# Odd channel tiles read in place, weight parts split one product ahead, and the last stores queued behind loads

## The chip, the cores and the metric

One core of one Trainium2 chip runs the kernel alone. The metric is the device time of one execution in microseconds (us), as the median of several runs.

## The reference

The reference is one decoder block in float32: attention and a gated recurrence side by side, an output projection, and an MLP with a squared ReLU. The change touches the MLP only:

```python
D_MODEL, SEQ, D_FF = 2048, 512, 8192
...
f = relu(h2 @ w_ff1) ** 2        # h2: 512 x 2048, the second norm's scaled output
x = x + gate2 * (f @ w_ff2)
```

## The kernel before

Every float32 product is made of three matmuls on values split into a high and a low part: high x high, high x low and low x high. A low part is `src - hi`; ACT casts the high one, DVE subtracts. `h2[k]` is the pair of high and low parts of channel tile k (128 channels x 512 tokens), k = 0 to 15, and `uT[k]` is the same tile unsplit. Both lie in SBUF.

The MLP's first 2048 hidden channels are computed plainly, in four groups (`first_hidden`, `hidden`), up to about 1190 us. All else is done in a form of Strassen's that needs seven products of half matrices in place of eight. For this the operands are stored in DRAM as seven *forms*: the quarters of `h2` and of `f`, and four sums of quarters. `input_forms` makes those of `h2` and `make_forms` those of `f`; each form has a high and a low half, in `h_hid` and `h_lod`, `f_hid` and `f_lod`. These stores are issued on POOL's queue (L1030).

Stage 1 computes the remaining hidden channels in six blocks of 1024 (b = 2 to 7), each of seven products numbered 1 to 7. Their order is 1, 5, 6, 7, 3, 4, 2; in the first block it is 1, 3, 5, 6, 7, 4, 2. Stage 2 multiplies `f` by `w_ff2` in two halves q of the output and four parts c, again seven products each. A product (`product`) is 48 matmuls of 128x512 into two PSUM banks: four steps u, each with 12 matmuls on one pair of weight parts `vhi`, `vlo`. `operand` fetches the other side's form, `Fh` and `Fl`, as two loads of 512 KB each for the high and for the low half, on POOL's queue from pools of four buffers each (L1097). For products 4 and 2 of stage 1 it loads four tiles of 1 MB (`Rh`, `Rl`) once and keeps them.

The weights come as `raw` tiles on SP's queue. `part` makes, where a product needs one, a difference of two raw tiles on DVE (L1129), casts it on ACT (`vhi`, L1145) and takes the low part on DVE (`vlo`, L1146):

```python
for u in range(KG):
    with tc.high_priority() if early else ExitStack():
        ws = part(i, u, w, first)
    mm(u, *ws, range(2))
    tick()
```

Each u has one buffer for its `vhi` and one for its `vlo`. After a product, `combine` adds its banks into the sums `s` (DVE L1204 to L1216, copies on ACT). `turn` transposes a finished group of f, applies the squared ReLU and stores its forms. In stage 2 the first part of each half copies the banks to `a` on ACT; behind the last copy, `residual_in` issues a `gate` load and eight `d` loads on ACT's queue.

A scheduler merges this program text into one order per engine, by priority; each engine runs its order in sequence. POOL's queue has eight lanes: an issue waits until the transfer issued eight before has landed.

Of the kernel before, what the change touches and what calls it, by code (L numbers as in the profile page):

```python
# [44 lines left out]
def hybrid_block(ctx, tc, x, c, positions, norm1_w, w_ada, b_ada, w_in, q_norm_w, k_norm_w,  # L45
# [177 lines left out]
    ph = ctx.enter_context(ExitStack())  # L223
    hp = ph.enter_context(tc.tile_pool(name="hp", bufs=1, side="right"))
# [15 lines left out]
    for i in range(NK):  # L240
        pair(i)
# [25 lines left out]
    spare.extend(hp.tile([P, 512], F32, name="araw", tag=f"{c}{k}") for k in range(8, NK) for c in ("hi", "lo"))  # L267
# [742 lines left out]
    def forms_in_dram(name, n):  # L1010
        return [dr.tile([n * FORMS * P, 512], F32, name=f"{name}_{c}d").rearrange("(g i p) n -> g i p n", i=FORMS, p=P)
                for c in ("hi", "lo")]

    fparts, hparts = forms_in_dram("f", NG), forms_in_dram("h", KG)

    def make_forms(fs, dst, g, stage, in_place=False):
# [7 lines left out]
        for a, b in ((0, 2), (2, 4), (4, 6), (6, 7)):  # L1024
            hi = stage()[:, 0:b - a]
            lo = fs[:, a:b].bitcast(F32R) if in_place else stage()[:, 0:b - a]
            act.copy(hi, fs[:, a:b])
            dve.tensor_tensor(lo, fs[:, a:b], hi.bitcast(F32), op=ALU.subtract)
            for d, t in zip(dst, (hi, lo)):
                pool.dma_start(d[g, a:b].rearrange("i p n -> p i n"), t.rearrange("p i a t -> p i (a t)").bitcast(F32))  # L1030
            yield
# [23 lines left out]
    for g in range(PLAIN):  # L1055
# [5 lines left out]
        for j, r in enumerate(rs):  # L1061
            dve.tensor_tensor(block(fs, j), halves(r), halves(r), op=ALU.mult)
# [9 lines left out]
    ph.close()  # L1072
# [307 lines left out]
```

## Time and profile before

| | us |
|---|---|
| median of 3 runs | 2312.09 (2311.49 to 2312.19) |
| profiled execution | 2306.17 |
| its span | 2304.4 |
| TensorE busy | 2230.5 (97%) |
| VectorE (DVE) busy | 1825.9 (79%) |
| ScalarE (ACT) busy | 1103.0 (48%) |
| mean granted clock | 0.994 |

Busy time is summed over the instructions of an engine. A timeline row gives start, duration, engine, source line, what is written and read, and in brackets the idle time ahead with what ended it. A chain of rows with `x3` has three instructions in one row. The clock is 1 at TensorE's upper level, 2.4 GHz, and a half at 1.2 GHz.

### The profile page before, as it was taken

Reading aid. Unit: us, or ns where it says so; the run is one execution under the profiler, and the core shown is the slowest. Engines: PE = TensorE matmul, PEld = TensorE weight load, DVE = VectorE, ACT = ScalarE, POOL = GpSimd, SP = SyncE. Lnnn points to the kernel's source line nnn. Section 1 sums busy time; section 2 is a strip of 40 time slices with the busy share of each in tenths; the row PEclk is TensorE's granted clock in tenths of the full one; section 3 lists DMA queues with packets and bytes.
Section 4 is the critical chain, followed back from the end, with each engine's and each line's share of the span. In section 5 each row is a group of like instructions: output and inputs, shape, how many; then the busy total and the mean of one; then the engine's idle time right before and its main releaser. Section 6 shows DMA issues by size and latency. Waiting matters only on the chain.

```text
span 2304.4 us, 33163 instructions
## 1 busy us (share of the span) xinstructions
PE 2230.5 (97%) x11769; PEld 1829.2 (79%) x11769; DVE 1825.9 (79%) x2773; ACT 1103.0 (48%) x1958; POOL 458.1 (20%) x668
## 2 busy tenths in 40 slices
PE   4999999999999999999999999999998999999999
PEld 3787877888778888888887888888887888888887
DVE  6899777677776565669767988988895789967878
ACT  5555434433344553457644555565563333344332
POOL 1000022000230000001332323323232222222221
PEclk9999999999999999999999999999999999999999
DMA  9798455556545256746999799889889987999784
GB/s 327 249 337 314 123 176 156 176 162 215 178 149 182 74 186 218 259 132 220 366 382 382 252 341 355 301 297 380 310 295 369 339 288 262 364 336 335 277 302 165
DMA packets 264695, 606.71 MB, mean 263 GB/s; under 512 B 23284, under 2 KB 44032, under 8 KB 264528
## 3 DMA queue, kind: packets, MB, share of 16 engines
q1 hardware_dynamic: 186800, 332.54, 42.8%
q0 software_dynamic: 72832, 262.60, 31.1%
q10 hardware_dynamic: 4896, 9.44, 1.2%
q8 instruction: 93, 1.52, 0.3%
q14 instruction: 74, 0.61, 0.1%
HBM read 522.68 MB, written 81.81 MB: 262 GB/s over the span
## 4 chain that ended last, share of the span: by engine, by line
PE 56%; DMA 16%; DVE 14%; issue 10%; POOL 2%; ACT 1%; SPq 0%; DVEq 0%; POOLq 0%; ACTq 0%
PE f L1160 9%; PE f L1161 9%; PE f L1159 9%; DMA araw<-in_w_ada_dram 7%; PE prj L198 4%; PE prj L200 4%; PE prj L199 4%; DMA f_lod<-fs 3%; DVE acc L129 3%; PE f L208 2%; PE f L206 2%; PE f L207 2%; DVE vlo L1146 2%; DVE wlo L40 2%; PE prj L206 2%
## 5 line engine op out<-in xcount | busy, mean ns | idle before, releaser
L1145 ACT CAST vhi<-raw 128x1024 fp32r<-128x1024 f32 x392 | 412.8, 1055 | 547.1 <-PE f L1161 434.3
L1146 DVE TENSOR_TENSOR vlo<-raw,vhi 128x1024 fp32r<-128x1024 f32 x392 | 477.4, 1225 | 154.3 <-ACT vhi L1145 153.5
L1159 PE MATMUL f<-vhi,Fh 128*128 128x512 f32 x1376 | 537.6, 391 | 8.3 <-DMA Fh<-h_hid 3.6
L1160 PE MATMUL f<-vlo,Fh 128*128 128x512 f32 x1376 | 538.1, 391 | 3.0 <-DVE vlo L1146 3.0
L1161 PE MATMUL f<-vhi,Fl 128*128 128x512 f32 x1376 | 537.2, 390 | 2.1 <-DMA Fl<-f_lod 1.3
L39 ACT CAST whi<-wraw 128x512 fp32r<-128x512 f32 (+1 forms) x368 | 219.8, 601 | 449.3 <-PE prj L200 323.7
L198 PE MATMUL prj<-whi,hi 128*128 128x512 f32 x896 | 365.0, 407 | 1.3 <-ACT gg L698 1.3
L200 PE MATMUL prj<-whi,lo 128*128 128x512 f32 x896 | 351.5, 392 | 0.0
L199 PE MATMUL prj<-wlo,hi 128*128 128x512 f32 x896 | 350.8, 391 | 0.0
L40 DVE TENSOR_TENSOR wlo<-wraw,whi 128x512 fp32r<-128x512 f32 (+1 forms) x368 | 245.1, 670 | 111.7 <-ACT whi L39 107.1
L129 DVE SCALAR_TENSOR_TENSOR acc<-araw,sc,acc 128x512 f32<-128x512 f32 (+1 forms) x392 | 253.9, 678 | 98.5 <-DMA araw<-in_w_ada_dram 97.2
L1159 PEld LDWEIGHTS f<-vhi,Fh 128*128 128x128 f32 x1376 | 259.0, 188 | 63.3 <-issue 7.1
L1160 PEld LDWEIGHTS f<-vlo,Fh 128*128 128x128 f32 x1376 | 259.0, 188 | 61.7 <-DVE vlo L1146 8.3
L1161 PEld LDWEIGHTS f<-vhi,Fl 128*128 128x128 f32 x1376 | 259.1, 188 | 56.7 <-DMA Fl<-f_lod 1.8
L1129 DVE TENSOR_TENSOR raw<-raw,raw 128x1024 f32<-128x1024 f32 x224 | 269.5, 1223 | 1.8 <-DMA raw<-in_w_ff_dram 1.5
L198 PEld LDWEIGHTS prj<-whi,hi 128*128 128x128 f32 x896 | 169.4, 189 | 36.5 <-ACT gg L698 1.6
L200 PEld LDWEIGHTS prj<-whi,lo 128*128 128x128 f32 x896 | 168.9, 188 | 36.8
L199 PEld LDWEIGHTS prj<-wlo,hi 128*128 128x128 f32 x896 | 169.6, 189 | 32.4 <-DVE wlo L40 0.4
L1097 POOL DMA_DIRECT2D Fh<-f_hid x112 | 80.9, 722 | 428.3 <-PE f L1161 414.8
L208 PE MATMUL f<-hi,wlo 128*128 128x512 f32 x256 | 99.8, 390 | 0.6 <-DVE wlo L40 0.6
L206 PE MATMUL f<-hi,whi 128*128 128x512 f32 x256 | 100.2, 391 | 0.0
L207 PE MATMUL f<-lo,whi 128*128 128x512 f32 x256 | 99.6, 389 | 0.0
(306 smaller groups left out, 2956.9 us busy)
## 6 DMA issues: line engine op xcount, KB each, us to landing
raw<-in_w_ff_dram SPq DMA_DIRECT2D x224, 512.0 KB, 10.0
araw<-in_w_ada_dram SPq DMA_DIRECT2D x384, 256.0 KB, 4.3
Fh<-f_hid POOLq DMA_DIRECT2D x112, 512.0 KB, 6.5
Fl<-f_lod POOLq DMA_DIRECT2D x112, 512.0 KB, 7.4
wraw<-in_w_in_dram SPq DMA_DIRECT2D x104, 512.0 KB, 4.1
Fh<-h_hid POOLq DMA_DIRECT2D x60, 512.0 KB, 6.8
Fl<-h_lod POOLq DMA_DIRECT2D x60, 512.0 KB, 8.3
f_hid<-part POOLq DMA_DIRECT2D x48, 512.0 KB, 8.1
```

What stands on the lines that cost most here:

```text
L39: nc.scalar.copy(hi, src)
L40: (eng or nc.vector).tensor_tensor(lo, src, hi.bitcast(F32), op=ALU.subtract)
L129: dve.scalar_tensor_tensor(acc, raw[:, k - k0], vec[:, k:k + 1], acc, op0=ALU.mult, op1=ALU.add)
L198: pe.matmul(banks[ti], lhsT=hi[:, ts], rhs=whi, start=first, stop=False)
L199: pe.matmul(banks[ti], lhsT=hi[:, ts], rhs=wlo, start=False, stop=False)
L200: pe.matmul(banks[ti], lhsT=lo[:, ts], rhs=whi, start=False, stop=last)
L1129: dve.tensor_tensor(dst, a, b, op=ALU.subtract)
L1145: act.copy(hi, src)
L1146: split_done.append(dve.tensor_tensor(lo, src, hi.bitcast(F32), op=ALU.subtract))
L1159: pe.matmul(banks[t], lhsT=fh[u][:, a, ts], rhs=whi[:, a], start=first, stop=False)
L1160: pe.matmul(banks[t], lhsT=fh[u][:, a, ts], rhs=wlo[:, a], start=False, stop=False)
L1161: pe.matmul(banks[t], lhsT=fl[u][:, a, ts], rhs=whi[:, a], start=False, stop=end)
```

## The change

Four things are done. The odd tiles of `h2` stay in SBUF (pool `hp1`) and products 4 and 2 of stage 1 read them there; the `R` tiles and their loads are gone. The forms of `h2` are made another way: of its quarters only one is stored, from the even tiles of `h2`, and the sums are taken by DVE out of `uT`, so the 16 copies on ACT go. The squares of the plain groups move from DVE to ACT. Last, one list of products (`items`) runs through both stages: inside each product the weight parts of the next one are split for u = 0 to 2 (`ahead`) and the fourth after the last product's combine; and the stores of the last turned group (`behind`) are issued after the operand loads that stand there.

```diff
@@ -220,8 +220,10 @@
...
-    ph = ctx.enter_context(ExitStack())
-    hp = ph.enter_context(tc.tile_pool(name="hp", bufs=1, side="right"))
+    ph1 = ctx.enter_context(ExitStack())
+    ph0 = ctx.enter_context(ExitStack())
+    hp1 = ph1.enter_context(tc.tile_pool(name="hp1", bufs=1, side="right"))
+    hp0 = ph0.enter_context(tc.tile_pool(name="hp0", bufs=1, side="right"))
...
-        return [hp.tile([P, S], F32R, name=f"{c}{i}", tag=f"{c}{i}") for c in ("hi", "lo")]
+        return [(hp0, hp1)[i % 2].tile([P, S], F32R, name=f"{c}{i}", tag=f"{c}{i}") for c in ("hi", "lo")]
...
-    for i in range(NK):
+    for i in (*range(0, NK, 2), *range(1, NK, 2)):
         pair(i)
...
@@ -1007,13 +1010,23 @@
...
-    fparts, hparts = forms_in_dram("f", NG), forms_in_dram("h", KG)
-
-    def make_forms(fs, dst, g, stage, in_place=False):
+    fparts, hparts = forms_in_dram("f", NG), forms_in_dram("h", KG, 8)
+
+    def split_out(fs, a, b, stage, in_place, dst, behind=None):
+
+        hi = stage()[:, 0:b - a]
+        lo = fs[:, a:b].bitcast(F32R) if in_place else stage()[:, 0:b - a]
+        act.copy(hi, fs[:, a:b])
+        dve.tensor_tensor(lo, fs[:, a:b], hi.bitcast(F32), op=ALU.subtract)
+        with tc.issue_after(behind[-1].ins) if behind else ExitStack():
+            for d, t in zip(dst, (hi, lo)):
+                pool.dma_start(d.rearrange("i p n -> p i n"), t.rearrange("p i a t -> p i (a t)").bitcast(F32))
+
+    def make_forms(fs, dst, g, stage, in_place=False, behind=None):
 
         a21, a11, a22, a12, s1, s2, s4 = (fs[:, i] for i in range(FORMS))
         dve.tensor_tensor(s1, a21, a22, op=ALU.add)
@@ -1022,12 +1035,7 @@
         dve.tensor_tensor(s4, a12, s2, op=ALU.subtract)
         yield
         for a, b in ((0, 2), (2, 4), (4, 6), (6, 7)):
-            hi = stage()[:, 0:b - a]
-            lo = fs[:, a:b].bitcast(F32R) if in_place else stage()[:, 0:b - a]
-            act.copy(hi, fs[:, a:b])
-            dve.tensor_tensor(lo, fs[:, a:b], hi.bitcast(F32), op=ALU.subtract)
-            for d, t in zip(dst, (hi, lo)):
...
     def plain_stage():
-        return stg.tile([P, 2, 2, 256], F32R, name="part", bufs=7)
...
     def input_forms(u):
-        fs = plain_forms()
-        for j in range(4):
-            act.copy(block(fs, j), halves(uT[4 * u + j]))
-        yield
-        yield from make_forms(fs, hparts, u, plain_stage)
+
+        xf = stg.tile([P, 4, 2, 256], F32, name="xf", bufs=1)
+        s1, s2, s4, s3 = (xf[:, i] for i in range(4))
+        for a in range(2):
+            ev, od = (halves(uT[4 * u + 2 * a + e]) for e in range(2))
+            a21, a11, a22, a12 = ev[:, 0], ev[:, 1], od[:, 0], od[:, 1]
+            dve.tensor_tensor(s1[:, a], a21, a22, op=ALU.add)
+            dve.tensor_tensor(s3[:, a], a11, a21, op=ALU.subtract)
+            dve.tensor_tensor(s2[:, a], s1[:, a], a11, op=ALU.subtract)
+            dve.tensor_tensor(s4[:, a], a12, s2[:, a], op=ALU.subtract)
+            for d, t in zip(hparts, h2[4 * u + 2 * a]):
+                pool.dma_start(d[u, 1, :, a * 256:(a + 1) * 256], t[:, 256:512].bitcast(F32))
+        yield
+        for a in (0, 2):
+            split_out(xf, a, a + 2, plain_stage, False, [d[u, 4 + a:6 + a] for d in hparts])
+            yield
...
         for j, r in enumerate(rs):
-            dve.tensor_tensor(block(fs, j), halves(r), halves(r), op=ALU.mult)
+            act.activation(block(fs, j), halves(r), AF.Square)
...
-    ph.close()
+    ph0.close()
...
     NC = NG // KG
-    kept = {}
 
     def operand(src, c, i):
 
-        def load(t, d, g):
-            n = t.shape[1]
-            pool.dma_start(t.rearrange("p g a t -> p g (a t)").bitcast(F32),
-                           d[g:g + n, slot_of[i]].rearrange("g p n -> p g n"))
-            return t
-
         if src is hparts and i in (4, 2):
-            if i not in kept:
-                kept[i] = [load(res.tile([P, KG, 2, 256], F32R, name=f"R{n}{i}"), d, 0) for d, n in zip(src, "hl")]
-            return [[t[:, u] for u in range(KG)] for t in kept[i]]
+            half = slice(256, 512) if i == 2 else slice(0, 256)
+            return [[[h2[4 * u + 2 * a + 1][j][:, half] for a in range(2)] for u in range(KG)] for j in range(2)]
         out_ = [[], []]
         for h in range(0, KG, 2):
             for o, d, n in zip(out_, src, "hl"):
-                t = load(pools["fp"].tile([P, 2, 2, 256], F32R, name=f"F{n}"), d, KG * c + h)
-                o.extend(t[:, u] for u in range(2))
+                t = pools["fp"].tile([P, 2, 2, 256], F32R, name=f"F{n}")
+                g = KG * c + h
+                slot_ = (hslot_of if src is hparts else slot_of)[i]
+                loads.append(pool.dma_start(t.rearrange("p g a t -> p g (a t)").bitcast(F32),
+                                            d[g:g + 2, slot_].rearrange("g p n -> p g n")))
+                o.extend([t[:, u, a] for a in range(2)] for u in range(2))
         return out_
 
     def weights(view, g0, c0, order):
...
-    def product(i, src, c, w, tag, by_tile, first, early):
+    def product(i, src, c, ws, tag, by_tile, nxt):
+
 
         banks = [bank("f2", tag=tag) for _ in range(2)]
         fh, fl = operand(src, c, i)
+        ahead = []
...
-                    pe.matmul(banks[t], lhsT=fh[u][:, a, ts], rhs=whi[:, a], start=first, stop=False)
-                    pe.matmul(banks[t], lhsT=fh[u][:, a, ts], rhs=wlo[:, a], start=False, stop=False)
-                    pe.matmul(banks[t], lhsT=fl[u][:, a, ts], rhs=whi[:, a], start=False, stop=end)
+                    pe.matmul(banks[t], lhsT=fh[u][a][:, ts], rhs=whi[:, a], start=first, stop=False)
+                    pe.matmul(banks[t], lhsT=fh[u][a][:, ts], rhs=wlo[:, a], start=False, stop=False)
+                    pe.matmul(banks[t], lhsT=fl[u][a][:, ts], rhs=whi[:, a], start=False, stop=end)
 
         if by_tile:
-            ws = [part(i, u, w, first) for u in range(KG)]
             for t in range(2):
                 for u in range(KG):
                     mm(u, *ws[u], (t,))
         else:
             for u in range(KG):
-                with tc.high_priority() if early else ExitStack():
-                    ws = part(i, u, w, first)
-                mm(u, *ws, range(2))
-                tick()
-        return banks
+                mm(u, *ws[u], range(2))
+                if u == KG - 1 or src is hparts:
+                    tick()
+                if nxt and u < KG - 1:
+                    ahead.append(nxt(u))
+        return banks, ahead
...
-        yield from make_forms(fs, fparts, 2 * b + n, stage, True)
+        yield from make_forms(fs, fparts, 2 * b + n, stage, True, loads if 2 * b + n == NG - 2 else None)
...
+    def part_of(item):
+
+        stage_, blk, j, i = item
+        if j == 0:
+            part_of.w = weights(ff1_s, 0, blk * 1024, order_of(item)) if stage_ == 1 else \
+                weights(ff2_s, blk[1] * KG, blk[0] * 1024, order)
+        w, first = part_of.w, blk == PLAIN // 2
+
+        def call(u):
+            with tc.high_priority() if first and j < 2 else ExitStack():
+                return part(i, u, w, first)
+        return call
+
+    def order_of(item):
+        return first_order if item[1] == PLAIN // 2 else order
+
+    items = [(1, b, j, i) for b in range(PLAIN // 2, NG // 2) for j, i in enumerate(order_of((1, b)))]
+    items += [(2, (q, c), j, i) for q in range(2) for c in range(NC) for j, i in enumerate(order)]
...
+    call = part_of(items[0])
+    ws = [call(u) for u in range(KG)]
+    for item, following in zip(items, items[1:] + [None]):
+        stage_, blk, j, i = item
+        first = blk == PLAIN // 2
+        if j == 0 and stage_ == 1 and not first:
+            before, cs, third = cs, after(cs), None
...
+            ph1.close()
+            late = ctx.enter_context(tc.tile_pool(name="late", bufs=1, side="right", reuse_waits="tile"))
...
+        if stage_ == 1:
+            banks, ahead = product(i, hparts, 0, ws, "bg" if first and j < 2 else "mm", False, call)
+            if i == 5 and not first:
+                turned(blk - 1, 0, before)
+            if first and i == 3:
+                third = banks
+            else:
                 for t in range(2):
...
+        else:
+            q, c = blk
+            banks, ahead = product(i, fparts, c, ws, "mm", i == 2 and c == NC - 1, call)
+            if q + c == 0 and i == 5:
+                turned(NG // 2 - 1, 0, cs)
+            for t in range(2):
+                if c == 0:
+                    done = act.copy(accs7[i, t], banks[t])
+                elif c < NC - 1:
+                    dve.tensor_tensor(accs7[i, t], accs7[i, t], banks[t], op=ALU.add)
+                else:
+                    finish(q, i, t, banks[t])
+            if c == 0 and i == 2:
                 with tc.issue_after(done.ins):
                     residual_in(q)
+        if following:
+            ws = ahead + [call(u) for u in range(len(ahead), KG)]
```

Three places show how the orders move. The first is POOL's order at the start of stage 1. `part` is a staged half of a form of f from the last plain group, `Fh` and `Fl` are operand loads, and the first eight of those belong to products 1 and 3. Before:

```order
L1097 DMA Fl<-h_lod 128x2x512
L1097 DMA Rh_12618<-h_hid 128x4x512
L1097 DMA Rl_12620<-h_lod 128x4x512
L1097 DMA Rh_12721<-h_hid 128x4x512
L1097 DMA Rl_12723<-h_lod 128x4x512
L1030 DMA f_hid<-part 128x2x512 x2
L1030 DMA f_lod<-part 128x2x512
L1030 DMA f_hid<-part 128x2x512
L1030 DMA f_lod<-part 128x2x512
L1030 DMA f_hid<-part 128x512
L1030 DMA f_lod<-part 128x2x512
L1097 DMA Fh<-h_hid 128x2x512
```

and now:

```order
L1122 DMA Fh<-h_hid 128x2x512
L1122 DMA Fl<-h_lod 128x2x512
L1027 DMA f_hid<-part 128x2x512
L1122 DMA Fh<-h_hid 128x2x512
L1122 DMA Fl<-h_lod 128x2x512
L1027 DMA f_hid<-part 128x2x512
L1027 DMA f_lod<-part 128x2x512 x2
L1027 DMA f_hid<-part 128x2x512
L1122 DMA Fh<-h_hid 128x2x512
L1122 DMA Fl<-h_lod 128x2x512
L1122 DMA Fh<-h_hid 128x2x512
```

The four `R` loads are gone, and one store, in place of seven, stands ahead of the pair that product 5 asks for first.

The second place is DVE's order in the first block, around product 7 and the following product 4. The numbers name tiles: `f_12530` and `f_12531` are product 7's banks before, `f_12518` and `f_12519` those of now; `vlo<-raw_12188`, `12190`, `12192`, `12194` are product 4's four low parts before, `raw_12156`, `12158`, `12160`, `12162` now. Before:

```order
L1129 TENSOR_TENSOR raw_12194<-raw_12194,raw_12218 128x1024
L1146 TENSOR_TENSOR vlo<-raw_12210,vhi 128x1024
L1146 TENSOR_TENSOR vlo<-raw_12188,vhi 128x1024
L1146 TENSOR_TENSOR vlo<-raw_12190,vhi 128x1024
L1146 TENSOR_TENSOR vlo<-raw_12192,vhi 128x1024
L1206 TENSOR_TENSOR s_12162<-s_12160,f_12530 128x512
L1206 TENSOR_TENSOR s_12163<-s_12161,f_12531 128x512
L1207 TENSOR_TENSOR s_12160<-s_12160,s_12146 128x512
L1207 TENSOR_TENSOR s_12161<-s_12161,s_12147 128x512
L1146 TENSOR_TENSOR vlo<-raw_12194,vhi 128x1024
L1208 TENSOR_TENSOR s_12146<-s_12146,s_12162 128x512
L1210 TENSOR_TENSOR s_12160<-s_12160,f_12296 128x512
```

and now:

```order
L1223 TENSOR_TENSOR s_12133<-s_12131,f_12518 128x512
L1161 TENSOR_TENSOR vlo<-raw_12156,vhi 128x1024
L1223 TENSOR_TENSOR s_12134<-s_12132,f_12519 128x512
L1224 TENSOR_TENSOR s_12131<-s_12131,s_12117 128x512
L1161 TENSOR_TENSOR vlo<-raw_12158,vhi 128x1024
L1144 TENSOR_TENSOR raw_12160<-raw_12160,raw_12184 128x1024
L1224 TENSOR_TENSOR s_12132<-s_12132,s_12118 128x512
L1225 TENSOR_TENSOR s_12117<-s_12117,s_12133 128x512
L1227 TENSOR_TENSOR s_12131<-s_12131,f_12280 128x512
L1144 TENSOR_TENSOR raw_12162<-raw_12162,raw_12186 128x1024
L1161 TENSOR_TENSOR vlo<-raw_12180,vhi 128x1024
L1225 TENSOR_TENSOR s_12118<-s_12118,s_12134 128x512
```

Three of the four low parts stood ahead of the combine that reads product 7's bank; now all four stand behind it, among the combines, the raw sums and the low parts of product 2 (`raw_12180` is one). The third, `vlo<-raw_12160`, follows two rows after the last one shown, behind one more combine.

The third place is POOL's order at the start of stage 2, with the stores of the last turned group (`part` and `fs`). Before:

```order
L1030 DMA f_hid<-part_16446 128x2x512
L1030 DMA f_hid<-part_16468 128x2x512
L1097 DMA Fh<-f_hid 128x2x512
L1097 DMA Fl<-f_lod 128x2x512
L1030 DMA f_lod<-fs_16369 128x2x512
L1030 DMA f_hid<-part_16490 128x2x512
L1030 DMA f_hid<-part_16524 128x512
L1030 DMA f_lod<-fs_16369 128x2x512 x2
L1030 DMA f_lod<-fs_16369 128x512
L1097 DMA Fh<-f_hid 128x2x512
L1097 DMA Fl<-f_lod 128x2x512
```

and now:

```order
L1027 DMA f_hid<-part_16532 128x2x512
L1027 DMA f_hid<-part_16616 128x2x512
L1122 DMA Fh<-f_hid 128x2x512
L1122 DMA Fl<-f_lod 128x2x512
L1027 DMA f_lod<-fs_16344 128x2x512 x2
L1122 DMA Fh<-f_hid 128x2x512
L1122 DMA Fl<-f_lod 128x2x512
L1027 DMA f_hid<-part_16698 128x2x512
L1027 DMA f_lod<-fs_16344 128x2x512
L1122 DMA Fh<-f_hid 128x2x512
L1122 DMA Fl<-f_lod 128x2x512
```

The group's stores, which stood together ahead of a pair of loads, now stand between the pairs.

## Rows read from the trace of the kernel before

**Rows 1.** The page, part 1: busy us, share of the span, instructions.

```profile
PE 2230.5 (97%) x11769; PEld 1829.2 (79%) x11769; DVE 1825.9 (79%) x2773; ACT 1103.0 (48%) x1958; POOL 458.1 (20%) x668
```

**Rows 2.** Windows: length, busy PE PEld DVE ACT POOL, PEclk, DMA share, GB/s.

```profile
1080.00:1189.80 109.80, 109.80 (x486) 90.93 (x485) 73.48 (x100) 58.56 (x90) 43.01 (x63) 1.00 1.00 373
1189.80:1290.00 100.20, 95.80 (x421) 78.44 (x420) 86.18 (x88) 48.85 (x56) 28.98 (x41) 0.98 0.96 356
...
1735.00:1776.00 41.00, 34.24 (x141) 27.00 (x140) 19.36 (x17) 15.12 (x18) 9.38 (x13) 0.96 1.04 392
```

**Rows 3.** Timeline of PE, 1207 to 1221 us: start, us, engine, line, operation.

```profile
1207.74 0.39 PE L1160 MATMUL f<-vlo,Fh 128*128 128x512 f32 x1
...
1211.37 0.39 PE L1161 MATMUL f<-vhi,Fl 128*128 128x512 f32 x1
1215.34 0.47 PE L1159 MATMUL f<-vhi,Fh 128*128 128x512 f32 x1 [3.58 <-DMA Fh<-h_hid]
...
1216.85 0.79 PE L1161 MATMUL f<-vhi,Fl 128*128 128x512 f32 x1 [0.81 <-DMA Fl<-h_lod]
...
1220.56 0.40 PE L1161 MATMUL f<-vhi,Fl 128*128 128x512 f32 x1
```

**Rows 4.** Timeline of POOL (DMA issues), 1178 to 1216 us.

```profile
1183.03 0.77 POOL L1097 DMA_DIRECT2D Rh<-h_hid  x1 [0.71 <-DMA Fh<-h_hid]
...
1190.29 0.75 POOL L1097 DMA_DIRECT2D Rl<-h_lod  x1 [1.96 <-PE f L208]
1195.58 0.71 POOL L1030 DMA_DIRECT2D f_hid<-part  x1 [4.54 <-ACT part L1027]
...
1206.00 0.73 POOL L1097 DMA_DIRECT2D Fh<-h_hid  x1 [1.95 <-DMA Rl<-h_lod]
1207.17 0.73 POOL L1097 DMA_DIRECT2D Fl<-h_lod  x1 [0.44 <-issue]
```

**Rows 5.** Waits of PE, 1080 to 1800 us: total, times, longest.

```profile
PE f L1160 <- DVE vlo L1146: 3.0, 7, 0.8
```

**Rows 6.** Timeline of PE at a block boundary of stage 1.

```profile
1291.68 0.50 PE L1160 MATMUL f<-vlo,Fh 128*128 128x512 f32 x1 [0.35 <-DVE vlo L1146]
```

**Rows 7.** Timeline of PE, 1738 to 1751 us.

```profile
1740.34 0.39 PE L1161 MATMUL f<-vhi,Fl 128*128 128x512 f32 x1
...
1745.46 0.50 PE L1161 MATMUL f<-vhi,Fl 128*128 128x512 f32 x1 [1.32 <-DMA Fl<-f_lod]
...
1749.16 0.44 PE L1161 MATMUL f<-vhi,Fl 128*128 128x512 f32 x1
```

**Rows 8.** Timeline of PE, 1769 to 1776 us.

```profile
1773.36 0.49 PE L1159 MATMUL f<-vhi,Fh 128*128 128x512 f32 x1 [1.96 <-ACT vhi L1145]
1774.62 0.50 PE L1160 MATMUL f<-vlo,Fh 128*128 128x512 f32 x1 [0.77 <-DVE vlo L1146]
```

**Rows 9.** Timeline of ACT and of its DMA issues (ACTq), 1760 to 1776 us.

```profile
1763.42 0.33 ACTq L1272 DMA_DIRECT2D gate<-gate  x1
...
1772.26 3.90 ACT L1145 CAST vhi<-raw 128x1024 fp32r<-128x1024 f32 x4 [8.39 <-DMA Fl<-f_lod]
```

**Rows 10.** Timeline of DVE, 1216 to 1253 us.

```profile
1217.61 1.23 DVE L1146 TENSOR_TENSOR vlo<-raw,vhi 128x1024 fp32r<-128x1024 f32 x1
...
1222.15 1.23 DVE L1146 TENSOR_TENSOR vlo<-raw,vhi 128x1024 fp32r<-128x1024 f32 x1
...
1245.55 3.49 DVE L1146 TENSOR_TENSOR vlo<-raw,vhi 128x1024 fp32r<-128x1024 f32 x3
...
1250.50 1.28 DVE L1206 TENSOR_TENSOR s<-s,f 128x512 f32<-128x512 f32 x2
1251.69 1.29 DVE L1207 TENSOR_TENSOR s<-s,s 128x512 f32<-128x512 f32 x2
```

**Rows 11.** Timeline of POOL, 1712 to 1745 us.

```profile
1732.05 0.73 POOL L1097 DMA_DIRECT2D Fl<-f_lod  x1 [1.20 <-DMA Fl<-f_lod]
```

**Rows 12.** DMA issues, section 6: count, KB each, median us to landing.

```profile
d<-x1d ACTq DMA_DIRECT2D x16, 256.0 KB, 9.6
```

More of the change, by code (lines that the diff above doesn't have):

```diff
@@ L266, in hybrid_block @@
     second_scale = mod_cols(1, 1, g1c, n1c, 256, True)
-    spare.extend(hp.tile([P, 512], F32, name="araw", tag=f"{c}{k}") for k in range(8, NK) for c in ("hi", "lo"))
+    spare.extend((hp0, hp1)[k % 2].tile([P, 512], F32, name="araw", tag=f"{c}{k}")
+                 for k in range(8, NK) for c in ("hi", "lo"))
     for _ in range(8):
@@ L1122, in weights @@
         return w
-    split_done = []
+    split_done, loads = [], []
     def sum_of(dst, a, b, first):
@@ L1210, in combine @@
                 dve.tensor_tensor(s6, s6, third[t], op=ALU.add)
-        if i == 3 and not third:
+        if i == 3:
             dve.tensor_tensor(s6, s6, b, op=ALU.add)
@@ L1226, in after @@
         return {1: cs[5], 5: cs[6], 6: cs[1], 7: cs[7]}
-    cs = {i: [s_[i, t] for t in range(2)] for i in (1, 5, 6, 7)}
-    for b in range(PLAIN // 2, NG // 2):
-        first = b == PLAIN // 2
-        w = weights(ff1_s, 0, b * 1024, first_order if first else order)
-        third = None
-        if not first:
-            before, cs = cs, after(cs)
-        for j, i in enumerate(first_order if first else order):
-            banks = product(i, hparts, 0, w, "bg" if first and j < 2 else "mm", False, first, first and j < 2)
-            if first and i == 3:
-                third = banks
-                continue
-            if i == 5 and not first:
-                turned(b - 1, 0, before)
-            for t in range(2):
-                combine(i, t, banks[t], cs, third)
-            if i == 4:
-                turned(b, 1, cs)
-    while len(tasks):
-        tick()
-    res_.close()
-    late = ctx.enter_context(tc.tile_pool(name="late", bufs=1, side="right", reuse_waits="tile"))
-    accs7 = {(i, t): late.tile([P, 512], F32, name=f"a{i}{t}") for i in (3, 4, 2) for t in range(2)}
-    for i, ts in after(cs).items():
-        for t in range(2):
-            accs7[i, t] = ts[t]
-    sums = {(r, n, t): late.tile([P, 512], F32, name=f"d{r}{n}{t}") for r in range(2) for n in range(2) for t in range(2)}
-    gates = []
     def gated(y, q, r, n, t):
@@ new lines, in order_of @@
+    def order_of(item):
+        return first_order if item[1] == PLAIN // 2 else order
+    items = [(1, b, j, i) for b in range(PLAIN // 2, NG // 2) for j, i in enumerate(order_of((1, b)))]
+    items += [(2, (q, c), j, i) for q in range(2) for c in range(NC) for j, i in enumerate(order)]
+    gates = []
+    cs = {i: [s_[i, t] for t in range(2)] for i in (1, 5, 6, 7)}
+    third = None
+    call = part_of(items[0])
[5 more added lines that the diff above has]
+            before, cs, third = cs, after(cs), None
+        if item == (2, (0, 0), 0, 1):
+            while tasks:
+                tick()
+            ph1.close()
+            late = ctx.enter_context(tc.tile_pool(name="late", bufs=1, side="right", reuse_waits="tile"))
+            accs7 = {(i, t): late.tile([P, 512], F32, name=f"a{i}{t}") for i in (3, 4, 2) for t in range(2)}
+            accs7 |= {(i, t): ts[t] for i, ts in after(cs).items() for t in range(2)}
+            sums = {(r, n, t): late.tile([P, 512], F32, name=f"d{r}{n}{t}")
+                    for r in range(2) for n in range(2) for t in range(2)}
+        call = part_of(following) if following else None
+        if stage_ == 1:
[5 more added lines that the diff above has]
+            else:
+                for t in range(2):
+                    combine(i, t, banks[t], cs, third)
+            if i == 4:
+                turned(blk, 1, cs)
+        else:
[11 more added lines that the diff above has]
+            if c == 0 and i == 2:
```

24 lines of the change are left out of this document (5 added, 19 removed).

## The prediction

> **What bounds the kernel now.** I read the page's busy shares first: TensorE is at work for 2230.5 us, 97% of the span [rows 1], so time can only be won where it stands still. Then the busy time by stretches: up to 1189.8 us the cover is complete (109.80 of 109.80 us), while in the first stage-1 block (1189.8 to 1290) 4.4 us are idle, and around the start of stage 2 (1735 to 1776) 6.8 us are, with the DMA engines full at a share of 1.04 [rows 2]. Last the timelines of PE and of the queue that it waits for. After 1080 us there are four kinds of loss; a matmul follows the last one by 0.227 us ((1211.37 - 1207.74)/16) [rows 3].
>
> - *First stall.* The third product of the first block (i=5) should start at 1211.60 and starts at 1215.34, waiting for `Fh` and then for `Fl` [rows 3]. From 1211.37 to 1220.56 there are 12 steps, worth 2.72 us, that take 9.19: 6.5 us lost. 1.7 of them come after the waits: the nine steps from 1216.85 take 3.71 instead of 2.04, with matmuls of 0.63 us, TensorE at its lower level of 1.2 GHz after idling 3.58 and 0.81 us.
> - *Its cause* is the POOL queue: the two loads were issued at 1206.00 and 1207.17, behind four `R` loads (1183.03 to 1190.29) and the `f` stores of the last hidden group, and the first of them waited for an `R` load [rows 4]. They took 9.3 and 9.7 us to arrive.
> - *Block boundaries.* Seven waits for `vlo`, 3.0 us in all [rows 5]; one, of 0.77, belongs to stage 2. The six others are like the one at 1291.68 with 0.35 us [rows 6].
> - *Second stall.* In stage 2, 12 steps from 1740.34 to 1749.16 take 8.82 us: 6.1 lost, 1.7 again at the lower clock [rows 7]. The awaited `Fl` stands in POOL's queue behind the turned group's stores.
> - *Third stall.* At 1773.36 and 1774.62 PE has idled 1.96 us for ACT and 0.77 for DVE [rows 8]. ACT had issued `gate` and eight `d` loads from 1763.42 and cast its next `vhi` only at 1772.26 [rows 9].
>
> **The change part by part.**
>
> *Work before 1189.8* (squares to ACT, 16 copies gone, sums by DVE out of `uT`, fewer stored forms, some stores straight from `h2`): at nothing, because PE is covered in every microsecond of that stretch, and both DVE (73.48 of 109.80) and ACT (58.56) have room [rows 2]. Uncovered, a square would be one more ACT pass of about 0.6 us ahead of a `vhi`.
>
> *First stall.* The four `R` loads vanish, and the pair that i=5 waits for moves from behind seven `f` stores to behind one. That store's cast came at 1195.58 on POOL [rows 4]; a microsecond or two later, with the squares in ACT's way, and the pair goes out by 1199. With the 9.7 us seen it lands by 1209, before 1211.6. **-6.5 us.** PE then asks 6.5 us earlier for the low parts. DVE's last one for i=5 ended in the trace at 1218.84 [rows 10], wanted at 1220.0; the first one for i=6 ended at 1223.38, wanted at 1222.7. So 0 to 0.7 us of a wait is left; I take 0.3, as at a block boundary [rows 6]. **+0.3.**
>
> *The order on DVE ahead of product i=4 in that block.* Before, three of i=4's four low parts stood ahead of the combines of i=7: DVE ran three low parts from 1245.55 (the last of i=7, two of i=4), one more of i=4, and then the combine at 1250.50 [rows 10]. Now the combine, which waits for the end of i=7 on PE, comes first, and each of i=4's low parts has combines and raw sums ahead of it. Two combines take 1.19 us (0.60 each); three wide operations take 3.49, one alone 1.23, so a step is 1.13 [rows 10]. From the end of i=7's first bank, PE can start i=4 after 0.5 us (three matmuls of the second bank are left) and wants its first low part at 0.75. That part is the second in DVE's line: 0.60 + 1.23 = 1.83, a wait of 1.1. The third low part is wanted 24 matmuls (5.44 us) on, at 7.3; ahead of it and with it stand eight combines and six wide ones, 4.8 + 6.8 = 11.6: a wait of 4.3. **+5.4 us.** After a wait of that length I put 1.7 more at the lower clock, as after 3.58 and 0.81 [rows 3]; the row against it is the third stall, where PE idled 1.96 and 0.77 and the next matmul took 0.50 us, not 0.63 [rows 8], so 0 is the other end. 4.3 is nearer to the first. **+1.7.** Nothing behind it gives this back: DVE only gains on PE in the meantime.
>
> *Block boundaries.* The orders on DVE and ACT from the second block to the last full one are the same row for row, though the program text says that weight parts are split earlier. **0**; the cover of all the others is unchanged.
>
> *Second stall.* POOL's queue moved 1732.05 (when the wait for an `Fl` ended) to 1745.46 (the late `Fl`) through seven units of 512 KB (halves counted as halves): 1.92 us a unit [rows 7, 11]. In the new order only two stores and the pair lie between: 1732.05 + 4 x 1.92 = 1739.7, wanted at 1741.0, so this wait goes. Two stores and the next pair follow: 1747.4, wanted at 1741.0 + 5.44 = 1746.45. So 0.9 of a wait is left, too short for the lower clock by the rows of the third stall. **-5.2.** The stores that now wait are read only by the fourth part of stage 2, hundreds of microseconds on.
>
> Here a rule speaks against the change. The pace of 1.92 us is 274 GB/s, 70% of the 392 that all queues moved [rows 2], so POOL's queue got more than an even share beside the weights' queue. The Trainium skill (DMA: Bandwidth & Descriptors, Queues, rings and completion order) says that a DMA engine takes turns between the queues that have work, packet by packet; with even turns 196 GB/s, 2.67 us a unit, would put the second pair at 1753.4, 7 us late, so that this term would be +0.9 and not -5.2 (2314.9 us). The trace has it otherwise, and I go by the trace.
>
> *Third stall.* The ACT order is unchanged. PE reaches it 5.2 us earlier, with the DMA engines still full, so ACT's wait for that transfer (8.4 us of idle ahead of the cast [rows 9]) can only grow; up to the `d` loads' median of 9.6 us [rows 12] it is +1.2. I take the upper part, **+1.0** (0 to 1.2).
>
> **Sum:** -6.5 + 0.3 + 5.4 + 1.7 - 5.2 + 1.0 = -3.3 us on the profiled execution's 2306.17, that is 2302.9. The median of the runs, 2312.09, stands 5.9 higher, so **2308.8 us**. With the ends: -6.3 (no 0.3, no 1.7, no 1.0) to -2.7 (0.7 and 1.2), 2305.8 to 2309.4. A measurement of this kernel can tell about 0.2%, 4.6 us, from no change.
>
> **Rivals.**
>
> *A, the DVE order does no harm*, because the high parts of i=4 or the sums reach DVE in time to be run in the gaps: -10.4, **2301.7 us**. For: the trace has no low part that waits so long behind a combine. Against: an engine that takes its rows in order can't run a low part ahead of a combine that waits.
>
> *B, the second stall's gain comes back*, since the DMA engines are full from 1735 to 1776 [rows 2], and what PE asks for earlier (weights, gate) arrives no earlier: +0.9, **2313.0 us**. For: the share of 1.04. Against: the stores put back are bytes that nobody needs there. The page's even turns would end near here too.
>
> *C, slower: DVE becomes the bound of the first block.* It is busy 86.18 of 100.20 us there [rows 2], and the block is to be 6 us shorter. If its low parts for i=5 come more than about 1.2 us later than in the trace, the first stall returns as waits for `vlo` (6.2 with what was saved, and 1.7 of clock): 0.9 + 6.2 + 1.7 - 4.2 = +4.6, **2316.7 us**. Against: the squares of the last hidden group leave DVE, so it should come earlier.
>
> **How the numbers follow.** Forecast 0.55 (0.20 of it below 2307.5), A 0.15, B 0.16, C 0.14 (0.10 of it above 2316.7). Faster by over 0.2%: 0.20 + 0.15 = 0.35; slower 0.10; within 0.55. The forecast's own range is 2305.8 to 2309.4; the range given reaches down to A and up to just under C, 2301.5 to 2316.0, and leaves out some 0.15.
>
> **What would show it.** Right: no wait for `h_hid` or `h_lod`; two waits for `vlo` in one product of about 1.1 and 4.3 us near 1245, with matmuls at 0.43 us a step behind the second; the wait for `f_lod` down to about 1 us; the wait for `vhi` after it 2 to 3 us; the six boundary waits as before. Wrong: a stage 2 that still loses 6 us or more before 1776 (B), many waits for `vlo` before product i=4 (C), or none in it (A).

## The result and the profile after

The changed kernel takes 2316.4 us (median of 15 runs, 2312.76 to 2321.41), the kernel before in the same comparison 2309.18 (15 runs): 1.0031 of it, 95% interval 1.002 to 1.0042, some 7 us slower. Forecast were 2308.8 and a range of 2301.5 to 2316.0. The forecast was 3.3 us less than the 2312.09 known then; against the 2309.18 of this comparison the change costs 7.2 us.

The profiled execution has a span of 2313.2 us, 8.8 more than before. Its busy times, part 1 of the page (compare [rows 1]):

```profile
PE 2229.1 (96%) x11769; PEld 1827.8 (79%) x11769; DVE 1811.0 (78%) x2765; ACT 1098.8 (48%) x1950; POOL 448.1 (19%) x664
```

What PE waited for from 1080 us on (engine and line, releaser, total, times, longest):

```profile
PE f L1176 <- ACT vhi L1160: 13.4, 1, 13.4
PE f L1177 <- DVE vlo L1161: 7.9, 9, 4.1
PE f L1178 <- DMA Fl<-f_lod: 0.2, 1, 0.2
```

The waits for `h_hid` and `h_lod` of [rows 3] are gone, and that for `Fl` in stage 2 has shrunk to 0.2 us. One wait of 13.4 us for a `vhi` stands in their place. The timeline of PE at the three places (columns as in [rows 3]):

```profile
1243.86 0.39 PE L1176 MATMUL f<-vhi,hi 128*128 128x512 f32 x1
1245.26 0.50 PE L1177 MATMUL f<-vlo,hi 128*128 128x512 f32 x1 [1.01 <-DVE vlo L1161]
...
1250.64 0.39 PE L1176 MATMUL f<-vhi,hi 128*128 128x512 f32 x1
1255.14 0.80 PE L1177 MATMUL f<-vlo,hi 128*128 128x512 f32 x1 [4.10 <-DVE vlo L1161]
...
1259.57 0.56 PE L1178 MATMUL f<-vhi,lo 128*128 128x512 f32 x1
...
1747.29 0.39 PE L1177 MATMUL f<-vlo,Fh 128*128 128x512 f32 x1
1747.92 0.50 PE L1178 MATMUL f<-vhi,Fl 128*128 128x512 f32 x1 [0.25 <-DMA Fl<-f_lod]
...
1766.42 0.39 PE L1178 MATMUL f<-vhi,Fl 128*128 128x512 f32 x1
1780.20 0.80 PE L1176 MATMUL f<-vhi,Fh 128*128 128x512 f32 x1 [13.40 <-ACT vhi L1160]
1781.46 0.80 PE L1177 MATMUL f<-vlo,Fh 128*128 128x512 f32 x1 [0.46 <-DVE vlo L1161]
...
1785.47 0.45 PE L1177 MATMUL f<-vlo,Fh 128*128 128x512 f32 x1
```

Subtract 0.227 from each step. In product 4 of the first block, 1.17 and 4.27 us are lost before the two `vlo`, and the ten steps up to 1259.57 take 4.43 in place of 2.27. In stage 2, 0.4 us is left of the second stall [rows 7]. The third stall [rows 8] had cost 2.1 + 1.0 us; now 13.55 and 1.03 are lost, and the nine steps behind them take 4.01 in place of 2.04. TensorE's clock is at its lower level after both long waits: the granted clock is 0.50 from 1255.1 to 1259.6 us and from 1780.2 to 1785.5, and the matmuls follow each other by 0.43 us.

| lost on PE, us | before | after |
|---|---|---|
| first stall (waits and lower clock) | 6.5 | 0 |
| product 4 of the first block | 0 | 7.6 |
| second stall | 6.1 | 0.4 |
| third stall | 3.2 | 16.6 |
| together | 15.8 | 24.6 |

8.8 us more. That the spans differ by the same 8.8 is in part chance: from the first matmul of stage 1 to the last one of the kernel it takes 9.8 us longer (1109.8 us before, 1119.6 after), and stage 1 began 1.0 us earlier. Where the third stall comes from is in ACT's timeline (ACTq are its DMA issues; `x8` are eight in one row, first start to last end):

```profile
1758.82 0.33 ACTq L1258 DMA_DIRECT2D gate<-gate  x1
1759.18 19.88 ACTq L1262 DMA_DIRECT2D d<-x1d  x8
1779.10 3.89 ACT L1160 CAST vhi<-raw 128x1024 fp32r<-128x1024 f32 x4 [19.83 <-DMA d<-x1d]
```

ACT issued `gate` and three `d` loads within 2 us, and then needed until 1779 for the other five. The `vhi` that PE wanted stood behind them. Before, ACT had issued all of them ahead of its cast at 1772.26 [rows 9]. The row `x8` hides where ACT stood. In narrow windows of the timeline its later issues have rows of their own, after the change:

```profile
1762.25 0.33 ACTq L1262 DMA_DIRECT2D d<-x1d  x1
1767.76 0.33 ACTq L1262 DMA_DIRECT2D d<-x1d  x1
1773.14 0.33 ACTq L1262 DMA_DIRECT2D d<-x1d  x1
1778.25 0.81 ACTq L1262 DMA_DIRECT2D d<-x1d  x2
```

and before, the sixth and the seventh of the eight:

```profile
1767.12 0.33 ACTq L1276 DMA_DIRECT2D d<-x1d  x1
1771.41 0.33 ACTq L1276 DMA_DIRECT2D d<-x1d  x1
```

So ACT stood between `d` loads in the kernel before too, until 1771.41.

### The profile page after: what moved, and what is told of

It is laid out like the page before. It is cut to its first block, busy times and chain, and to the rows that moved or that the text cites. A ratio compares the mean times of both kernels' runs of the same rounds, so it can differ in the third digit from the quotient of the medians.

```text
span 2313.2 us, 33104 instructions
## 1 busy us (share of the span) xinstructions
PE 2229.1 (96%) x11769; PEld 1827.8 (79%) x11769; DVE 1811.0 (78%) x2765; ACT 1098.8 (48%) x1950; POOL 448.1 (19%) x664
## 4 chain that ended last, share of the span: by engine, by line
PE 61%; DMA 13%; DVE 12%; issue 9%; POOL 2%; ACT 2%; SPq 0%; DVEq 0%; ACTq 0%; POOLq 0%
PE f L1177 10%; PE f L1178 10%; PE f L1176 10%; DMA araw<-in_w_ada_dram 6%; PE prj L198 5%; PE prj L200 5%; PE prj L199 5%; DVE acc L129 3%; PE f L208 2%; PE f L207 2%; PE f L206 2%; DVE wlo L40 2%; PE prj L207 1%; PE prj L206 1%; PE prj L208 1%
## 5 line engine op out<-in xcount | busy, mean ns | idle before, releaser
L1161 DVE TENSOR_TENSOR vlo<-raw,vhi 128x1024 fp32r<-128x1024 f32 x392 | 476.1, 1221 | 170.9 <-ACT vhi L1160 170.0
L1176 PE MATMUL f<-vhi,Fh 128*128 128x512 f32 x1376 | 537.1, 390 | 13.4 <-ACT vhi L1160 13.4
```

Of the source, the lines that this page charges most:

```text
L1161: split_done.append(dve.tensor_tensor(lo, src, hi.bitcast(F32), op=ALU.subtract))
L1176: pe.matmul(banks[t], lhsT=fh[u][a][:, ts], rhs=whi[:, a], start=first, stop=False)
```

## The experiments

The theory to be tested (L): a `d` load waits until its lane's last transfer has landed, ACT stands meanwhile, and five of the lanes were last used by weight loads of part c=1. The program shows the five, of which the lane's earlier user is a `raw` load on SP's queue:

```
L1262 DMA d_16185<-x1d 128x512 [waits DMAHW4_49]
L1262 DMA d_16186<-x1d 128x512 [waits DMAHW5_49]
L1262 DMA d_16187<-x1d 128x512 [waits DMAHW6_49]
L1262 DMA d_16188<-x1d 128x512 [waits DMAHW7_49]
L1262 DMA d_16189<-x1d 128x512 [waits DMAHW0_49]
...
L1136 DMA raw_16733<-in_w_ff_dram 128x2x512 [waits DMAHW5_49,DVE_49]
L1136 DMA raw_16735<-in_w_ff_dram 128x2x512 [waits DMAHW6_49,DVE_49]
L1136 DMA raw_16737<-in_w_ff_dram 128x2x512 [waits DMAHW7_49,DVE_49]
L1136 DMA raw_16739<-in_w_ff_dram 128x2x512 [waits DMAHW0_49,DVE_49]
```

The trace bears this out. The last four weight loads of the part were issued at 1741.44, 1744.16, 1746.88 and 1750.09 us and landed at 1762.23, 1767.73, 1773.12 and 1778.23; the fourth to seventh `d` load, on the same four lanes, were issued at 1762.25, 1767.76, 1773.14 and 1778.25. (The first of the five lanes was free in time, at 1758.3, and the eighth `d` load waits for the gate's.) The last weight load was issued at 1755.22 us before and at 1750.09 after. Its time to landing (DMA issues of that moment: count, KB each, us), before:

```profile
raw<-in_w_ff_dram SPq DMA_DIRECT2D x1, 512.0 KB, 16.2
```

and after:

```profile
raw<-in_w_ff_dram SPq DMA_DIRECT2D x1, 512.0 KB, 28.1
```

It landed at 1771.4 before and at 1778.2 after, each time just ahead of the seventh `d` load. Issued 5.1 us earlier, it landed 6.8 us later. The rival (B) is the one of the forecast: the DMA engines are full, so PE loses the time wherever the loads stand.

The part of the kernel up to 1190 us, which the change hardly alters for PE, varies by some 8 us between executions (the first wait of product 4 begins between 1242.7 and 1250.8 us), so the table compares the time that PE lost after 1080 us: the sum of what the steps from one matmul to the next exceed 0.227 us by, over all that exceed it by more than 0.15 us.

| kernel | lost after 1080 us | time, us |
|---|---|---|
| before | 18.7 | 2309.18 |
| after | 28.9 | 2316.4, ratio 1.0031 (1.002 to 1.0042) |
| e1, residual's loads called later | 25.9 | 2315.26, 1.0029 (1.0017 to 1.004) |
| e2 and g3, on SP's queue | 11.8 and 11.6 | 2301.66, one run, and 2300.47, 0.9965 (0.9948 to 0.9983) |
| e3, small `d` loads | 29.9 | 2319.51, one run |
| e4, stores ahead again | 19.2 | 2305.33, one run |
| f1, combine behind | 22.2 | 2311.31, one run |
| f2, before, loads on SP | 16.5 | 2304.78, one run |
| f3, loads behind c=1's casts | 12.1 | 2304.33, one run |
| f4, on SP, and combine behind | 6.8 | 2294.25, 0.9943 (0.9926 to 0.996) |
| g1, before with the stores behind | 25.9 | 2314.68, 1.0028 (1.0012 to 1.0044) |
| g2, the same, loads on SP | 9.7 | 2299.23, 0.9964 (0.9949 to 0.9979) |
| h1, on SP, in the same stretch | 12.7 | 2303.9, 0.9976 (0.9961 to 0.9992) |

**e1, the loads called one part later.**

```diff
             if c == 0 and i == 2:
-                with tc.issue_after(done.ins):
+                copied = done
+            if c == 1 and i == 2:
+                with tc.issue_after(copied.ins):
                     residual_in(q)
```

> The gate load and the eight d loads of each half are issued behind part c=1 and not behind c=0. Theory L (lanes): ACT stands still because five d loads use a lane whose last transfer, a weight load of the next part, has not landed yet; a part later those have landed, so the wait of 13.4 us for vhi shrinks to under 3 us and the time falls by 12 to 17 us, to about 2300. Theory B (bandwidth): the DMA engines are full after c=0 and something has to be late; PE then waits about as long for weights or operands, and the time falls by under 4 us.

It did not test what it was meant to: the scheduler put the loads back to their old place, one `vhi` later, and PE waited 10.4 us. A later call in the program text is not a later issue.

**e2, the loads on SP's queue** (and **g3**, the same kernel run ten times).

```diff
-        act.dma_start(gates[q], gate2[:, q * 1024:(q + 1) * 1024].rearrange("o (n c) -> o n c", n=2)
+        nc.sync.dma_start(gates[q], gate2[:, q * 1024:(q + 1) * 1024].rearrange("o (n c) -> o n c", n=2)
...
-            act.dma_start(d, x1d[:, ti, cs].rearrange("p o n -> p (o n)"))
+            nc.sync.dma_start(d, x1d[:, ti, cs].rearrange("p o n -> p (o n)"))
```

> The same nine loads at the same place of the program, issued on SP's queue in place of ACT's. Theory L: ACT casts go on, so the wait for vhi at 1780 falls from 13.4 to under 2 us; SP stands instead, behind weight loads that nobody needs yet. Theory B: the bytes are the same, so PE loses still over 8 us there, now waiting for weights or for Fh and Fl.

> The changed kernel with the residual's loads on SP's queue, timed in rounds: by its one look some 13 us less than the changed kernel, so 2300 to 2305, 2 to 4 us more than with the combine repaired too would be if that repair were worth less than its trace shows, 7 us more if it is worth what the trace shows.

What PE waited for in e2:

```profile
PE f L1177 <- DVE vlo L1161: 7.4, 8, 4.1
PE f L1178 <- DMA Fl<-f_lod: 0.6, 1, 0.6
```

The wait for `vhi` is gone and nothing took its place: 17.1 us less is lost. But the expectation's "same place" did not hold: on SP the scheduler issued the `d` loads before stage 2 (1678 to 1686 us), so their bytes had left the full stretch as well. h1 mends this.

**e3, small `d` loads.**

```diff
-            act.dma_start(d, x1d[:, ti, cs].rearrange("p o n -> p (o n)"))
+            act.dma_start(d[:, 0:16], x1d[:, ti, cs].rearrange("p o n -> p (o n)")[:, 0:16])
...
+            if q + c == 0 and i == 3:
+                for d in sums.values():
+                    dve.memset(d, 0.0)
```

> The d loads keep their place on ACT's queue but fetch 16 of 512 columns (the rest of the residual is left out and set to zero by DVE), so 2 MB less per half moves. Theory L: the d loads still wait for the lanes of the weight loads, which land somewhat sooner without the 2 MB beside them; the wait for vhi is 6 to 11 us. Theory B: with the bytes gone the wait falls under 3 us.

ACT's timeline in e3:

```profile
1766.85 16.96 ACTq L1262 DMA_DIRECT2D d<-x1d  x8
1783.85 3.89 ACT L1160 CAST vhi<-raw 128x1024 fp32r<-128x1024 f32 x4 [16.92 <-DMA d<-x1d]
```

With 1/32 of the bytes ACT still took 17 us for the eight issues, and PE waited 10.2 us. It is not the residual's own transfer that ACT waits for. The bytes still count for something: the wait is 3.2 us shorter than with all of them. That PE's total is no smaller comes from the added `memset`s, which hold DVE for 3.2 us at 1688.46 and make PE wait 1.8 us for a `vlo` at 1692.78.

**e4, the stores ahead again.**

```diff
-        yield from make_forms(fs, fparts, 2 * b + n, stage, True, loads if 2 * b + n == NG - 2 else None)
+        yield from make_forms(fs, fparts, 2 * b + n, stage, True)
```

> Only the order of the last turned group's stores is undone: they stand ahead of the operand loads again. Both theories: the wait for f_hid and f_lod of about 6 us near 1745 comes back (0.25 us in the changed kernel). Theory L: PE and ACT then reach the d loads about 6 us later, the weight loads have landed further, and the wait for vhi falls from 13.4 to 2 to 6 us, so that the sum is smaller by 2 to 6 us. Theory B: the wait for vhi falls by what is lost before, no more than 6 us, and the time stays within 2 us.

What PE waited for in e4:

```profile
PE f L1177 <- DVE vlo L1161: 8.0, 9, 4.1
PE f L1176 <- DMA Fh<-f_hid: 2.3, 1, 2.3
PE f L1178 <- DMA Fl<-f_lod: 1.2, 1, 1.2
```

The second stall is back (2.3 and 1.2 us of idling), and the wait of 13.4 us is gone altogether, where theory L had let 2 to 6 us of it stay and theory B over 7. ACT's issues in e4:

```profile
1764.91 6.40 ACTq L1262 DMA_DIRECT2D d<-x1d  x8
1771.36 1.99 ACT L1160 CAST vhi<-raw 128x1024 fp32r<-128x1024 f32 x2 [6.36 <-DMA gate<-gate]
```

The last weight load of the part, issued at 1756.3, landed here after 12.3 us, at 1768.7. So PE's second stall had not been pure loss: with PE late, POOL issued nothing from 1742.7 to 1753.6 us, and the weight loads came through. Without the stall the same transfer takes 28.1 us.

**f1, product 7's combine behind product 4's low parts.**

```diff
-                for t in range(2):
-                    combine(i, t, banks[t], cs, third)
+                with tc.issue_after(split_done[-1].ins) if first and i == 7 else ExitStack():
+                    for t in range(2):
+                        combine(i, t, banks[t], cs, third)
```

> One line: in the first block the combine of product 7 is issued behind the third low part of product 4, so DVE's order there is again as before the change. Theory O (order): the two waits for vlo of 1.0 and 4.1 us in product 4 and the lower clock behind them come from the combine's place alone; they go, 7 us less up to 1290, and the wait of 13 us behind c=0 stays within 3 us of what it was. Theory D (DVE is short of time in this block): waits for vlo of 3 us or more turn up in product 4 or 2 all the same.

PE's waits:

```profile
PE f L1176 <- ACT vhi L1160: 12.6, 1, 12.6
PE f L1177 <- DVE vlo L1161: 2.7, 7, 0.5
PE pt L1206 <- DVE s L1225: 0.9, 1, 0.9
```

Both waits in product 4 are gone; the seven `vlo` waits left are the six boundaries and one in stage 2. 0.9 us turns up later, at a transpose that waits for a combine. Net 6.7 us less lost. The order alone was the cause.

That order does not come from splitting weight parts ahead. With that part of the change undone (the parts split inside the product that uses them), the order of all five engines is the same, row for row, as in the changed kernel; it was not timed. Which part of the change moved the combine was not tested. I take it that the scheduler, which places the rows by its own estimate of when they are ready, estimates otherwise with the `R` loads gone.

**f2, the kernel before with the loads on SP's queue**, by e2's edit.

> The kernel before, with only the gate and d loads on SP's queue. Theory L: its waits for Fh and Fl near 1215 and 1743 stay as they were (6.5 and 6.1 us lost) and the third stall (1.96 and 0.77) goes: 2 to 4 us less than before. If the loads on SP by themselves were what makes the version with them there fast, 8 us or more would go.

PE's waits:

```profile
PE f L1159 <- DMA Fh<-h_hid: 3.0, 1, 3.0
PE f L1159 <- DMA Fh<-f_hid: 2.6, 1, 2.6
...
PE f L1161 <- DMA Fl<-f_lod: 0.6, 1, 0.6
```

The first two stalls stay, the third is gone; 2.2 us less is lost. Moving the loads is worth little by itself, so e2's gain in the changed kernel is the repair of what the change broke.

**f3, the loads on ACT's queue, behind the casts of part c=1.**

```diff
-        act.copy(hi, src)
+        casts.append(act.copy(hi, src))
...
-            if c == 0 and i == 2:
-                with tc.issue_after(done.ins):
+            if c == 1 and i == 2:
+                with tc.issue_after(casts[-1].ins):
                     residual_in(q)
```

> The gate and d loads stay on ACT's queue, but behind the last cast for part c=1 of each half. Theory L: no wait for vhi of over 1 us behind c=0; behind c=1 ACT can stand behind weight loads of c=2, but the queues are no longer full there, so under 5 us. Theory B: the transfers cost PE as much wherever they lie, over 8 us.

ACT's issues:

```profile
1838.71 5.95 ACTq L1262 DMA_DIRECT2D d<-x1d  x8
1844.76 2.95 ACT L1160 CAST vhi<-raw 128x1024 fp32r<-128x1024 f32 x3 [5.50 <-DVE raw L1144]
```

ACT stood for 6 us and PE did not wait at all, behind c=0 or behind c=1. The engine and the bytes are those of the changed kernel; only the weight loads were in another state. Since the place is another too, this run alone does not decide between L and B.

**f4, both repairs** (e2's and f1's edits).

> The changed kernel with both repairs: the residual's loads on SP's queue and product 7's combine behind the low parts. If both are independent, 13 us from the first and 7 us from the second: 2316 - 20, about 2296, 0.994 of the kernel before. If the earlier PE only meets the next shortage in stage 2, the second repair is worth under 3 us and the time stays near 2301.

PE's waits:

```profile
PE f L1177 <- DVE vlo L1161: 2.2, 6, 0.4
PE f L1178 <- DMA Fl<-f_lod: 1.2, 1, 1.2
PE pt L1206 <- DVE s L1225: 1.2, 1, 1.2
```

The repairs add, but for 1.7 us: 28.9 - 17.1 - 6.7 = 5.1 was to be lost, and 6.8 is. At 2294.25 us and a ratio of 0.9943 this version beats both kernels.

**g1, the kernel before with only the stores moved.** `loads` and `behind` as in the change, and in stage 2 a background step only behind the last u of a product.

```diff
                 mm(u, *ws, range(2))
-                tick()
+                if u == KG - 1 or src is hparts:
+                    tick()
...
-        yield from make_forms(fs, fparts, 2 * b + n, stage, True)
+        yield from make_forms(fs, fparts, 2 * b + n, stage, True, loads if 2 * b + n == NG - 2 else None)
```

> The kernel before with only the last group's stores placed between the operand loads, as the change does it (the stores issued behind the loads, and in stage 2 one background step per product in place of four). Theory L: the wait for Fh and Fl near 1743 (6.1 us lost) falls to about 1 us, the wait for vhi behind it grows from 1.96 to 10 to 14 us with the lower clock behind it: 6 to 10 us slower than before. If the moved stores only pay when PE comes as early as in the changed kernel, the wait for vhi stays under 4 us and the kernel is 4 to 6 us faster.

PE's waits:

```profile
PE f L1161 <- ACT vhi L1147: 12.2, 1, 12.2
PE f L1161 <- DMA Fh<-h_hid: 3.0, 1, 3.0
...
PE f L1163 <- DMA Fl<-f_lod: 0.8, 1, 0.8
```

The moved stores, with the fewer background steps that go with them, make the kernel before slower without the rest of the change, 1.0028 of it, with the same 12 us for `vhi` in place of the second stall.

**g2, the same with the loads on SP's queue.**

> The same kernel with the gate and d loads on SP's queue besides. Theory L: both stage-2 stalls are gone, so it is 6 to 9 us faster than before; the first block's wait for Fh and Fl (6.5 us) stays. Theory B: a wait of over 5 us turns up at another place before 1790.

9.7 us lost, ratio 0.9964: with ACT out of the way the moved stores are a gain. The first stall, untouched here, is still 3.0 and 0.6 us of idling.

**h1, the loads on SP's queue, behind the last weight load of the next part.**

```diff
-                    nc.sync.dma_start(raw, view[:, g0 + u, e, :, c0 + n * 512:c0 + (n + 1) * 512])
+                    raws.append(nc.sync.dma_start(raw, view[:, g0 + u, e, :, c0 + n * 512:c0 + (n + 1) * 512]))
...
-                with tc.issue_after(done.ins):
+                with tc.issue_after(raws[-1].ins):
                     residual_in(q)
```

> The gate and d loads on SP's queue, and tied behind the last weight load of part c=1, so that their bytes move in the stretch where the changed kernel moved them (in the first version on SP the scheduler had put the d loads before stage 2). Theory L: ACT's casts go on, no wait for vhi of over 2 us behind c=0, and the kernel is 11 to 15 us faster than the changed one, as with the d loads before stage 2. Theory B: the same bytes in the same full stretch cost PE over 8 us of waits before 1800.

SP's timeline in h1:

```profile
1757.52 23.23 SPq L1264 DMA_DIRECT2D d<-x1d  x8
```

and PE's waits:

```profile
PE f L1179 <- DVE vlo L1163: 7.4, 8, 4.1
PE f L1180 <- DMA Fl<-f_lod: 0.7, 1, 0.7
```

SP now needs 23 us for the same eight issues, in the same full stretch, and PE waits for none of it: the `vlo` waits are those of the first block and of the boundaries. This separates L from B. The same bytes issued in the same stretch are harmless when the engine that stands behind the weight loads is one that nobody waits for. They do land later (1782 to 1795 us in place of 1769 to 1782), behind the weights on SP's queue, but the DMA engines are as full: 387 GB/s from 1764 to 1776 us, against 389 in the changed kernel. The median of 2303.9 lies above e2's; the time lost after 1080 us is within 1 us of it, and the part ahead of product 4 varies by more than the medians differ, so I read no difference between the two.

## Why the prediction was wrong, step by step

- **First stall, -6.5: right.** No wait for `h_hid` or `h_lod` is left. The +0.3 set against it is there where it was looked for, at the first low part of i=6: a step of 0.49 us at 1221.66, 0.26 lost.
- **Product 4 of the first block, +5.4 and +1.7: right.** 1.17 and 4.27 us against 1.1 and 4.3, and about 2 us for the lower clock. f1 shows that the order is the cause. Rival A (the order does no harm) falls.
- **Block boundaries, 0: right.** Six waits of 0.37 to 0.40 us, as in [rows 6].
- **Second stall, -5.2: right, slightly better.** 0.4 us is left, 0.9 was forecast. The even turns that the prediction sets against this term do hold, packet by packet: from 1735 to 1750 us the trace before counts 1084 packets of POOL's queue and 1082 of SP's. But a packet of POOL's carried 3.6 KB on average and one of SP's 1.9 KB, so POOL's queue moved 65% of the bytes. The +0.9 came from taking even turns for even bytes.
- **Third stall, +1.0: wrong, it is +13.4.** This is the step that failed: "up to the `d` loads' median of 9.6 us [rows 12] it is +1.2". I took ACT's wait to be for a transfer of its own queue, the gate's, and bounded its growth by how long such loads take. Already before the change the wait that ended last was for a weight load: it landed at 1771.39 and the seventh `d` load was issued at 1771.41, while the gate had landed at 1770.96. In [rows 9] that is hidden, since the eight issues are one row and the idle time is put down to an `Fl`. The bound had to be the landing of the last weight load, and that came 6.8 us later. With ACT at the loads 4.6 us earlier (1758.82 for 1763.42) this makes 11.4, by which PE's wait for `vhi` grew (1.96 to 13.40); the other 2.0 are the lower clock behind it.
- **Rival B had the right stretch and the wrong size.** It let the second stall's 6.1 us come back. More came back than was won, 13.4 us for 5.7, because the weights did not only arrive no earlier but later. The bytes alone do not cost that time either: in h1 they cost PE nothing.
- **Sum.** With 13.4 in place of 1.0 the forecast's -3.3 becomes +9.1; the spans differ by 8.8.
- Rival C (DVE the bound of the first block) did not happen: ahead of product 4 no wait for `vlo` cost more than the 0.26 us above.

The Trainium skill (DMA: Bandwidth & Descriptors, Issuing engines are not separate DMA queues) says that starting transfers from several engines saves only the time in which a sequencer starts them. For what the DMA engines move the runs agree: 389 GB/s with the loads on ACT's queue, 387 in h1 (1764 to 1776 us). For the time they do not: which engine issued nine loads was worth about 13 us (1.0031 against 0.9976), because that engine also had the casts to do.

## What to carry to other kernels

Before a stall is removed, list what else waits on the same transfers. The program's wait lists name the lanes, and narrow windows of the timeline show which issue stood until which landing; a merged row like the `x8` of ACT's loads hides it. An engine with work on the critical path should not issue loads that can stand behind somebody else's transfers; give them to a queue on which nothing urgent follows. And check after each change where the scheduler has put the rows: here a later call did not mean a later issue (e1), and splitting parts earlier in the text changed no engine's order.

## What the runs showed that I had not expected

- The last weight load of part c=1 took 16.2 us to land before and 28.1 after, with the DMA engines full in both (a share of 1.04 from 1735 to 1776 us [rows 2] and, in the changed kernel, from 1764 to 1776). What differs is who takes turns. The packets, MB and shares of the DMA queues (q0 is POOL's, q1 SP's, q10 ACT's), from 1754 to 1762 us before:

```profile
q1 hardware_dynamic: 804, 1.55, 53.2%
q0 software_dynamic: 430, 1.54, 50.4%
```

and after:

```profile
q0 software_dynamic: 558, 2.02, 66.5%
q1 hardware_dynamic: 559, 1.08, 37.3%
```

and after, from 1764 to 1776 us, with ACT's loads under way:

```profile
q0 software_dynamic: 624, 2.27, 49.4%
q10 hardware_dynamic: 623, 1.28, 28.9%
q1 hardware_dynamic: 579, 1.11, 25.7%
```

Queues that all have work move about as many packets each. Before, POOL's queue had run dry behind the second stall, and the weights moved 194 GB/s. After, they had every second packet (135 GB/s), and from then on every third (93 GB/s): ACT's own loads slowed the weights that ACT was waiting for. Where ACT's loads lie elsewhere (e2, f3, f4, g2, g3, h1) the last weight load takes 23.0 to 24.9 us, so by this estimate some 3 to 5 of the 13.4 us come from the loads' own bytes.

- A lane is shared by SP's and ACT's queues: `d` loads issued by ACT waited for weight loads issued by SP, and with 1/32 of the bytes they still took 17 us to be issued.
- Taking away a stall of 6 us by a few moved stores (g1) made the kernel 0.28% slower.

What stays open is why a packet of POOL's queue carries nearly twice the bytes of the others, and which part of the change moved the combine of product 7.
